# Token projections of 512 columns instead of 256, PSUM banks four/two/two, and another order of the linear attention

## The chip, the core and the metric

The kernel runs on one core of a Trainium2 chip. The metric is the device time of one launch in microseconds, from the runs' median. Engines are named as the profile names them: PE (TensorE, with PEld its weight loads), DVE (VectorE), ACT (ScalarE), POOL (GpSimd) and SP (SyncE, which issues most of the DMAs here).

## What is computed

Two transformer blocks over 512 tokens of width 1024, all in float32. The first block is a bidirectional gated linear attention (eight heads) beside a spatial gating unit; the second is a mixer (pooling beside an attention over the best 128 keys of each query), a cross attention over 256 memory tokens, and a mixture of 32 experts. Cut to the projections that the change touches:

```python
# block 1
proj = jnp.einsum('bsd,de->bse', _rmsnorm(x, norm_w), w_in)        # 10 splits of 1024 columns
(q, f_fwd, f_bwd, i, ga, u, v, gb, ma, mb) = jnp.split(proj, split_points, axis=-1)
y_a = _hgrn2_branch(q, f_fwd, f_bwd, i, ga, ...)                   # values i, output gate silu(ga)
y_b = _spatial_gating_branch(u, v, gb, ...)                        # layernorm(gelu(v))
merged = sigmoid(ma) * (y_a @ w_proj_a) + sigmoid(mb) * (y_b @ w_proj_b)
x = rmsnorm(x + merged @ w_out)
# block 2
z = rmsnorm(x) @ w_in_2                   # pooled part, q, k, v of 512 each, qi 512, ki 64, wi 8
q = apply_rope(rmsnorm(q)); k = apply_rope(rmsnorm(k)); qi = apply_rope(qi)
score = einsum(relu(qi @ ki), wi);  sel = top_k(score, 128)
x = x + concat([pool_mixer(u), attention(q, k[sel], v[sel])]) @ w_out_2
x = x + softmax(rmsnorm(h @ xattn_wq) @ rmsnorm(m @ wkv_k).T) @ (m @ wkv_v) @ xattn_wo
x = x + mixture_of_experts(rmsnorm(x))    # 2 experts per token of 32
```

## The kernel before

**Products.** A float32 product is made of three fp32r products (`mm3`, L152 to L155): both operands are split into a rounded part (`_h`) and the rest (`_l`), and high by high, high by low and low by high are summed in PSUM. There are two forms. `proj_T` (L166) holds a 128 by 128 block of the weights and moves all 512 tokens past it. `proj_tok` (L172) holds a block of 128 tokens and moves columns of the weights past it, 256 columns in the kernel before: two token tiles share one PSUM tile of 512 columns. The values of the linear attention (`gla_proj`, products `pi`), its gates (`gla_gate`, `pg`), the gating input (`sg_input`, `pv`), the memory's keys and values (`kv_unit`, `pkv`), both output projections (`pwo`, `pwo2`), the mixer's indexer queries, keys, queries and values (`qk_unit`: `pqi`, `pk`, `pq`; `v_unit`: `pvv`) and the cross attention's queries (`xq_unit`, `pxq`) have the second form. For each token tile and block of 256 columns there are 8 contraction blocks of 128, so 24 products.

**Weights.** `load_w` (L137) fetches 256 columns of a 1024-row matrix as two DMAs of 512 KB from SP's queue into a ring of two raw tiles; ACT rounds each to its high part (L131), and DVE, in two places POOL, subtracts for the low part (L132). High and low tiles have rings of two as well, so one block of weights is in use while the next one is made.

**PSUM.** The eight banks are given to three tags (L157 to L164): three `mm` for projections, three `sm` for scores, sums and the like, two `tp` for transposes.

**Order.** The source order is the priority; the framework's scheduler, which times instructions by a model of its own, writes one fixed order for each engine, and each engine then runs its own order and waits for others by semaphores. Steps that wait for other engines (the transposes of normalised queries) are postponed: they are kept in `pend` and emitted by `flush` behind later projections.

**Linear attention** (L242 to L408, main loop under `sg_input`): for each pair of heads `gla_proj` makes values, forget gates and queries, `gla_gate` the output gates of the pair; `gla_scores` builds each head's decayed scores by doublings (DVE and POOL products of decays, ACT and PE in turn), `gla_out` sums the values (`po`), normalises and gates them.

**Mixer attention.** `qk_unit` projects 256 columns of two token tiles, squares on ACT, sums on DVE (L534), takes the inverse root on POOL (L124, L125), multiplies on DVE (L536) and rotates on DVE (L649) and POOL (L653, L658). `score` (L747) adds up the indexer's scores on DVE (L757 to L760); `topk` (L763) takes the best 128 in rounds of a MAX8 (L767) and a MATCH_REPLACE8 (L768), 16 rounds for each of the query tiles 1 to 3, all on DVE. `attend` (L838) uses the selection.

**Experts.** 16 rounds of two experts, whose weights stream from HBM into buffers that earlier rounds free (L967 issues from SP).

Of the kernel before, what the change touches and what calls it, by code (L numbers as in the profile page):

```python
# [4 lines left out]
F32 = mybir.dt.float32  # L5
# [17 lines left out]
def host_consts():  # L23
    """Arrays that depend on the shapes alone: identity, masks, counters, rotary tables."""
# [37 lines left out]
def program(tc, I, out, sb, ps, dr, dbg, upto):  # L62
# [58 lines left out]
    def rstd_of(ss, n, k, eps, name):  # L121
        """(ss / n + eps) ** -0.5 on a small [128, k] tile."""
# [5 lines left out]
    def split(src, hi, lo, gain=None, eng=None):  # L128
        """hi + lo = src (times a gain per partition), hi rounded to fp32r."""
# [7 lines left out]
    def load_w(src, c0, n, name, kb=8, dst=None, eng=None):  # L137
        """Columns c0..c0+n of a [kb*128, *] matrix as fp32r hi and lo."""
# [12 lines left out]

    def mm3(o, ah, al, bh, bl, first=True, last=True):  # L152
# [13 lines left out]
    def proj_T(o, w, c0, act, kb=8, m=128):  # L166
        """o[c, t] = sum_d w[d, c0+c] act[d, t] (weights stationary)."""
# [4 lines left out]
    def proj_tok(o, act, i, w, c0, n, ks, kw=None, first=True, last=True):  # L172
        """o[t, c] over token tile i (tokens stationary), contraction blocks ks of act."""
# [6 lines left out]
    def to_T(src, i, dst, nk=8):  # L180
        """Transpose token tile src [128, nk*128] into dst hi/lo [:, k, i*128:]."""
# [13 lines left out]
    def norm_tile(dst, src, wb, name, eps=1e-6):  # L195
        """dst = rmsnorm(src) * wb for one token tile [128, 1024]."""
# [6 lines left out]
    # ================= block 1 =================  # L203
    w_in = I["w_in"][0]
    w_first = load_w(w_in, 3 * D, 256, "wi0", eng=nc.gpsimd)
# [8 lines left out]
    # forget gate bounds: lb = cumsum(softmax(lower_bounds, layers)) - first, one layer  # L214
# [25 lines left out]
    st = {}  # L240

    def gla_proj(h):  # L242
        hp, j = divmod(h, 2)
        c0 = h * 128
        if j == 0:
            wv = load_w(w_in, 3 * D + hp * 256, 256, f"wi{hp}") if hp else w_first
            for ip in range(2):
                p = pmm(f"pi{hp}_{ip}")
                for ii in range(2):
                    proj_tok(p[:, ii * 256:(ii + 1) * 256], hT, 2 * ip + ii, wv, 0, 256, range(8))  # L250
                nc.scalar.activation(V[:, 2 * ip:2 * ip + 2, hp * 256:(hp + 1) * 256],
                                     p.rearrange("p (i c) -> p i c", i=2), AF.Copy)
# [3 lines left out]
            # G slots: 0 q bwd, 1 k fwd, 2 q fwd, 3 k bwd, 4.. scores; T slots: 0 bwd, 1 fwd  # L256
# [24 lines left out]

    def gla_gate(hp):
        wg = load_w(w_in, 4 * D + hp * 256, 256, f"wga{hp}")
        gate = s4(f"gate{hp}", (128, 4, 256))
        for ip in range(2):
            p = pmm(f"pg{hp}_{ip}")
            for ii in range(2):
                proj_tok(p[:, ii * 256:(ii + 1) * 256], hT, 2 * ip + ii, wg, 0, 256, range(8))
            gv = gate[:, 2 * ip:2 * ip + 2, :]
            pv = p.rearrange("p (i c) -> p i c", i=2)  # L290
            nc.scalar.activation(gv, pv, AF.Sigmoid)
            nc.vector.tensor_tensor(gv, gv, pv, OP.mult)
        st["gate", hp] = gate

    def gla_scores(h):
        G, T, q = st[h]
        # products of the decays over blocks of m positions, at 1024 + 2 * (512 - 2 * 512 / m)
# [25 lines left out]
        def put(src, other, copy):  # L323
            """These blocks' places in the scores."""
# [5 lines left out]
        # queries with their own position's decay  # L330
# [5 lines left out]
        def widen(m):  # L336
            """from blocks of m to blocks of 2m"""
# [27 lines left out]
        # the other 128s, through the sums of keys times values that reach each of the four from either side  # L365
# [46 lines left out]
    def sg_input():  # L412
        """LayerNorm(gelu(v)) in token layout"""
        vn = a16("vn", F32, (128, 4, 1024))
        for c in range(4):
            w = load_w(w_in, 6 * D + c * 256, 256, f"wv{c}")
            for ip in range(2):
                p = pmm(f"pv{c}_{ip}")
                for ii in range(2):
# [1043 lines left out]
```

## Time and profile before

| | |
|---|---|
| median of 3 runs | 1339.22 us (1337.23 to 1342.84) |
| the profiled execution | span 1338.4 us; its time stands 0.8 us below the median |
| granted TensorE clock | 0.993 of full speed in the mean |
| PE, DVE, ACT, POOL busy | 1299.5, 774.1, 494.6, 210.3 us |
| DMA | 207.67 MB, 155 GB/s in the mean |

The stages follow one another: start and first norms to 66 us, linear attention and gating input to 375, merge and gating to 605 and memory keys and second half of the merge to 667, output projection to 713, mixer projections to 794, selection and attention to 898, mixer output and cross attention to 1071, experts to the end. An engine's busy time is read stage by stage, since each has its own limit, and an operation's duration differs from its pitch: a product's record of 0.28 us overlaps the next one's, and the distance of two starts is what a product costs.

### The profile page before, as it was taken

Reading aid. Unit: us, or ns where it says so; the run is one execution under the profiler, and the core shown is the slowest. Engines: PE = TensorE matmul, PEld = TensorE weight load, DVE = VectorE, ACT = ScalarE, POOL = GpSimd, SP = SyncE. Lnnn points to the kernel's source line nnn. Section 1 sums busy time; section 2 is a strip of 40 time slices with the busy share of each in tenths; the row PEclk is TensorE's granted clock in tenths of the full one; section 3 lists DMA queues with packets and bytes.
Section 4 is the critical chain, followed back from the end, with each engine's and each line's share of the span. In section 5 each row is a group of like instructions: output and inputs, shape, how many; then the busy total and the mean of one; then the engine's idle time right before and its main releaser. Section 6 shows DMA issues by size and latency. Waiting matters only on the chain. (4 is left out here: it accounts for less than half of the span.)

```text
span 1338.4 us, 22160 instructions
## 1 busy us (share of the span) xinstructions
PE 1299.5 (97%) x8998; PEld 1058.0 (79%) x8998; DVE 774.1 (58%) x1458; ACT 494.6 (37%) x853; POOL 210.3 (16%) x254
## 2 busy tenths in 40 slices
PE   6999999999999999999999999899999999999997
PEld 5898989899988888888899868757898846666553
DVE  4467676666662345444456479993447735555544
ACT  4355454646431343433433334355435211111110
POOL 2202011030010000100002465361011110000000
PEclk9999999999999999999999999899999999999999
DMA  6322222222423332234642322231198599999995
GB/s 187 95 81 78 65 65 84 75 64 64 158 79 95 110 106 83 80 95 142 197 141 76 95 71 64 64 108 66 64 296 305 191 309 362 359 358 357 362 361 195
DMA packets 178699, 207.67 MB, mean 155 GB/s; under 512 B 14711, under 2 KB 155767, under 8 KB 178593
## 3 DMA queue, kind: packets, MB, share of 16 engines
q1 hardware_dynamic: 171808, 197.91, 45.7%
q10 hardware_dynamic: 4624, 4.44, 1.1%
q0 software_dynamic: 2160, 3.85, 0.9%
q8 instruction: 73, 1.20, 0.4%
q14 instruction: 34, 0.27, 0.1%
HBM read 201.81 MB, written 8.39 MB: 157 GB/s over the span
## 5 line engine op out<-in xcount | busy, mean ns | idle before, releaser
L1302 PE MATMUL pgu<-gu,hgT 128*64 128x256 f32 (+1 forms) x944 | 116.3, 398 | 3.6 <-DMA gu<-in_expert_w_up 3.6
L1302 PEld LDWEIGHTS pgu<-gu,hgT 128*64 128x64 f32 x944 | 70.4, 137 | 50.0 <-issue 6.8
L353 ACT ACTIVATE qk<-G 128x512 f32<-128x512 f32 x112 | 69.1, 666 | 51.6 <-DVE G L343 51.6
L1341 DVE TENSOR_TENSOR fx<-fx,pad 128x512 f32<-128x512 f32 x128 | 77.9, 678 | 1.0 <-PE pad L1340 1.0
L1326 PE MATMUL pdn<-dn,sh 128*64 128x512 f32 x256 | 61.6, 604 | 0.0
L1307 DVE SCALAR_TENSOR_TENSOR sh<-sh,grs,pgu 128x256 f32<-128x256 f32 x16 | 7.7, 480 | 87.5 <-ACT sh L1306 87.5
L340 DVE TENSOR_TENSOR G<-G,T 128x512 f32<-128x512 f32 x56 | 39.2, 700 | 31.4 <-ACT qk L353 28.6
L1339 PE MATMUL pad<-yh,put 128*128 128x512 f32 x128 | 52.9, 417 | 0.9 <-DVE fx L1341 0.9
L1340 PE MATMUL pad<-yl,put 128*128 128x512 f32 x128 | 49.9, 394 | 0.0
L131 ACT ACTIVATE yh<-pdn 128x512 fp32r<-128x512 f32 x32 | 19.1, 597 | 73.0 <-PE pdn L1326 73.0
L1306 ACT ACTIVATE sh<-pgu,grs 128x256 f32<-128x256 f32 x16 | 7.6, 474 | 103.9 <-PE pgu L1302 103.9
L1275 POOL DMA_INDIRECT hg<-x3d,lst_i x15 | 15.1, 1008 | 184.7 <-PE thg L1284 171.4
L153 PE MATMUL pi<-wi_h,hT_h 128*128 128x256 f32 x128 | 38.1, 298 | 3.3 <-ACT hT_h L131 2.3
L304 POOL TENSOR_TENSOR T<-T 128x512 f32<-128x512 f32 (+6 forms) x56 | 31.3, 560 | 54.1 <-DVE T L271 50.4
L132 DVE TENSOR_TENSOR yl<-pdn,yh 128x512 fp32r<-128x512 f32 x32 | 22.1, 691 | 30.2 <-ACT yh L131 30.2
L343 DVE TENSOR_TENSOR G<-G,T 128x512 f32<-128x512 f32 x56 | 38.8, 692 | 0.0
L154 PE MATMUL pi<-wi_l,hT_h 128*128 128x256 f32 x128 | 38.0, 297 | 0.2 <-POOL wi_l L132 0.2
L155 PE MATMUL pi<-wi_h,hT_l 128*128 128x256 f32 x128 | 37.6, 294 | 0.0
L1326 PEld LDWEIGHTS pdn<-dn,sh 128*64 128x64 f32 x256 | 15.7, 136 | 27.5 <-issue 26.4
L153 PE MATMUL pv<-wv_h,hT_h 128*128 128x256 f32 x128 | 36.8, 288 | 0.0
L153 PE MATMUL pg<-wga_h,hT_h 128*128 128x256 f32 x128 | 36.7, 287 | 0.0
L155 PE MATMUL pv<-wv_h,hT_l 128*128 128x256 f32 x128 | 36.7, 287 | 0.0
(542 smaller groups left out, 4142.3 us busy)
## 6 DMA issues: line engine op xcount, KB each, us to landing
gu<-in_expert_w_gate SPq DMA_DIRECT2D x32, 1024.0 KB, 12.4
gu<-in_expert_w_up SPq DMA_DIRECT2D x32, 1024.0 KB, 12.6
dn<-in_expert_w_down SPq DMA_DIRECT2D x44, 512.0 KB, 9.7
wo_r<-in_w_out SPq DMA_DIRECT2D x16, 512.0 KB, 3.5
wq_r<-in_w_in SPq DMA_DIRECT2D x12, 512.0 KB, 3.7
dn<-in_expert_w_down SPq DMA_DIRECT2D x5, 1024.0 KB, 8.5
dn<-in_expert_w_down SPq DMA_DIRECT2D x20, 256.0 KB, 8.3
wi_r<-in_w_in SPq DMA_DIRECT2D x8, 512.0 KB, 4.9
```

What stands on the lines that cost most here:

```text
L153: nc.tensor.matmul(o, ah, bh, start=first, stop=False)
L154: nc.tensor.matmul(o, ah, bl, start=False, stop=False)
L155: nc.tensor.matmul(o, al, bh, start=False, stop=last)
L304: nc.gpsimd.tensor_tensor(ap_of(T, o, [[n2, 2], [1, n2]]), ap_of(T, a, [[sa, 2], [2, n2]]), ap_of(T, a + 1, [[sa, 2], [2, n2]]), OP.mult)
L340: nc.vector.tensor_tensor(ap_of(G, 0, [[512, 2], [2 * m, nb], [1, m]]), ap_of(G, 0, [[512, 2], [2 * m, nb], [1, m]]), ap_of(T, a + 1, [[sa ...
L343: nc.vector.tensor_tensor(ap_of(G, 1024 + m, [[512, 2], [2 * m, nb], [1, m]]), ap_of(G, 1024 + m, [[512, 2], [2 * m, nb], [1, m]]), ap_of( ...
L353: nc.scalar.activation(ap_of(qk, a * 512, [[2 * m, nb], [m, 2], [1, m]]), ap_of(G, a * 512, [[2 * m, nb], [1024 + m, 2], [1, m]]), AF.Copy)
L1302: nc.tensor.matmul(pg[m * a:m * a + m, c0:c0 + n], hT_[:, k, m * a:m * a + m], t[:, k, :], start=k == 0 and c0 == 0, stop=k == 7 and c0 + ...
L1326: nc.tensor.matmul(po[m * a:m * a + m, :], hd[:, f, m * a:m * a + m], dn[f][:, hs], start=f == 0, stop=f == 1)
L1339: nc.tensor.matmul(p, pi, yh[:, hs], start=True, stop=False)
L1340: nc.tensor.matmul(p, pi, yl[:, hs], start=False, stop=True)
L1341: V_.tensor_tensor(fx[:, i, hs], fx[:, i, hs], p, OP.add)
```

## The change

Every projection of the second form moves 512 columns of weights instead of 256. `load_half` fetches four contraction blocks of 512 columns (two DMAs of 512 KB, as before, but each of two blocks by 512 columns); `tok512` goes through the lower four contraction blocks for all token tiles and then through the upper four, so each token tile holds a PSUM bank of its own from its first product to its last. `pmm` has four banks and `psm` two. `done` empties a tile's bank. A gate projection serves four heads and is emptied as two halves of 256 columns. In the linear attention each `gla_scores(h)` is followed in the source by an independent projection: gates of four heads, the other values, or the gating input. The memory's keys come behind the second block of the merge and its values behind the fourth. In the mixer a unit is one token tile of 512 columns, and the indexer's scores of query tiles 1 and 2 follow the key tiles 2 and 3. Cut to its core:

```diff
+    def load_half(src, c0, b, name, eng=None, dst=None, kb=8):
+        ncol = src.shape[1]
+        if dst is None:
+            dst = (sb.tile([128, 4, 512], F32R, name=f"{name}_h{b}", tag="wh", bufs=2),
+                   sb.tile([128, 4, 512], F32R, name=f"{name}_l{b}", tag="wl", bufs=2))
+        hi, lo = dst
+        for q in range(2):
+            raw = sb.tile([128, 2, 512], F32, name=f"{name}_r{b}{q}", tag="wr", bufs=2)
+            nc.sync.dma_start(raw, bass.AP(tensor=src.tensor, offset=src.offset + c0 + (4 * b + 2 * q) * 128 * ncol,
+                                           ap=[[ncol, 128], [128 * ncol, 2], [1, 512]]))
+            split(raw, hi[:, 2 * q:2 * q + 2], lo[:, 2 * q:2 * q + 2], eng=eng)
+        return hi, lo
+
+    def tok512(src, c0, act, name, done, order=None, nt=4, eng=None, halves=None):
+        p, w = {}, halves or {}
+        for b, i in order or [(b, i) for b in range(2) for i in range(nt)]:
+            if b not in w:
+                w[b] = load_half(src, c0, b, name, eng)
+            if b == 0:
+                p[i] = pmm(f"p{name}_{i}")
+            proj_tok(p[i], act, i, w[b], 0, 512, range(4 * b, 4 * b + 4), range(4), first=b == 0, last=b == 1)
+            if b == 1:
+                done(i, p[i])
...
-        return ps.tile([128, 512], F32, name=name, tag="mm", bufs=3)
+        return ps.tile([128, 512], F32, name=name, tag="mm", bufs=4)
...
-        return ps.tile([128, 512], F32, name=name, tag="sm", bufs=3)
+        return ps.tile([128, 512], F32, name=name, tag="sm", bufs=2)
...
+        def done(i, p):
+            for a in range(2):
+                gv, pv = gates[a][:, i, :], p[:, a * 256:(a + 1) * 256]
+                nc.scalar.activation(gv, pv, AF.Sigmoid)
+                nc.vector.tensor_tensor(gv, gv, pv, OP.mult)
+        tok512(w_in, 4 * D + hp * 256, hT, f"wga{hp}", done)
...
+    gla_values(0)
     gla_proj(0)
     for h in range(0, 8, 2):
-        gla_gate(h // 2)
+        if h % 4 == 0:
+            gate_tiles(h // 2)
         gla_scores(h)
+        if h % 4 == 0:
+            gla_gate(h // 2)
+        elif h == 2:
+            gla_values(1)
+        else:
+            sg_cols(0)
         gla_out(h)
         gla_scores(h + 1)
         if h < 6:
             gla_proj(h + 2)
         else:
-            sg_input()
+            sg_cols(1)
+            sg_norm()
         gla_out(h + 1)
...
-        if c > 0:
-            kv_unit(c - 1)
+        if c % 2:
+            kv_unit(c // 2)
...
+    def k_after(i):
+        flush(2)
+        if i > 1:
+            score(i - 1)
+
+    qk_units(1024, "k", rk, True, put_k, between=k_after)
...
     score(3)
-    for c in range(2):
-        wq = load_qk(512, c, "q")
-        for ip in range(2):
-            qk_unit(wq, c, ip, "q", rq, True, put_q)
-            flush(1)
+    qk_units(512, "q", rq, True, put_q, between=lambda i: flush(1))
```

`qk_units` has the steps of `qk_unit` for one token tile and 512 columns; `load_w4` and `proj_w4` do the same for the two output projections, and `xq_done` for the cross attention's queries. Three places of the fixed orders follow; the numbers at the end of a name tell instances apart.

**PE, first head's sum over the values** (`pkv0`, `po0`; `pf` and `pf2`, `pf3` are forget gates of the next heads, `pwga` the gates of the change; rows that only repeat are left out). Before:

```order
L378 MATMUL pkv0_0_760<-V_199,kt0_748 128x128 x3
L378 MATMUL pkv0_1_767<-V_199,kt0_748 128x128 x3
L395 MATMUL po0_774<-V_199,G0_330 128x128
L154 MATMUL pf3_1_1124<-hT_l_86,wfb1_h_1061 128x512
L155 MATMUL pf3_1_1124<-hT_h_85,wfb1_l_1062 128x512
L153 MATMUL pf3_1_1124<-hT_h_85,wfb1_h_1061 128x512
```

And with the change:

```order
L180 MATMUL pwga0_3_726<-wga0_l1_740,hT_h_95 128x512
L181 MATMUL pwga0_3_726<-wga0_h1_739,hT_l_96 128x512
L404 MATMUL pkv0_0_663<-V_209,kt0_651 128x128 x3
L404 MATMUL pkv0_1_670<-V_209,kt0_651 128x128 x3
L421 MATMUL po0_813<-V_209,G0_344 128x128
L425 MATMUL po0_813<-sm0_652,G0_344 128x128
L423 MATMUL po0_813<-sm0_652,G0_344 128x128
L179 MATMUL pf2_1_1024<-hT_h_95,wfb1_h_990 128x512
L180 MATMUL pf2_1_1024<-hT_l_96,wfb1_h_990 128x512
```

Before, projections of the next pair of heads stand between the sums; with the change the sums follow the gates' last products with no projection between, and the next projection `pf2_1` needs an `mm` bank, of which the gate tiles hold all four until they are emptied.

**PE, start of the first output projection** (`pwo`, weights `wo`). Before:

```order
L154 MATMUL pkv3_5781<-wkv3_l_5772,mmT_4972 128x256
L155 MATMUL pkv3_5781<-wkv3_h_5771,mmT_4972 128x256
L153 MATMUL pwo0_0_5881<-wo0_h_5839,mT_h_5753 128x256
L154 MATMUL pwo0_0_5881<-wo0_l_5840,mT_h_5753 128x256
L155 MATMUL pwo0_0_5881<-wo0_h_5839,mT_l_5754 128x256
```

And with the change:

```order
L180 MATMUL pwkv1_1_5108<-wkv1_l1_5122,mmT_4412 128x512
L179 MATMUL pwo0_0_0_5225<-woa_h0_5183,mT_h_5157 128x512
L179 MATMUL pwo0_0_1_5251<-woa_h0_5183,mT_h_5157 128x512
L180 MATMUL pwo0_0_0_5225<-woa_l0_5184,mT_h_5157 128x512
L181 MATMUL pwo0_0_0_5225<-woa_h0_5183,mT_l_5158 128x512
L180 MATMUL pwo0_0_1_5251<-woa_l0_5184,mT_h_5157 128x512
L181 MATMUL pwo0_0_1_5251<-woa_h0_5183,mT_l_5158 128x512
```

Before, one token tile runs through all its blocks in a row; with the change two tiles take turns at the pace of the weight blocks, here after 12 products of each 512 KB.

**DVE, first selection** (`m8_1_r` is round r of query tile 1; `sc1` and `ksc` are scores, `qn` the queries' norms). Before:

```order
L768 MATCH_REPLACE sc1_6401<-m8_1_2_7479,sc1_6401 128x256
L759 SCALAR_TENSOR_TENSOR ksc_6400<-rl2_3_7109,wi_6728,ksc_6400 128x384
L536 TENSOR_TENSOR qn0_0_7246<-pq0_0_7197,qn0_0_r_7250 128x512
L767 MAX m8_1_3_7482<-sc1_6401 128x8
L759 SCALAR_TENSOR_TENSOR ksc_6400<-rl2_4_7114,wi_6728,ksc_6400 128x384
```

And with the change:

```order
L797 MAX m8_1_0_6329<-sc1_5545 128x8
L569 TENSOR_TENSOR qn2_6279<-pwq_2_6175,qn2_r_6283 128x512
L798 MATCH_REPLACE sc1_5545<-m8_1_4_6341,sc1_5545 128x256
L567 TENSOR_REDUCE qn3_q_6312<-qn3_6310 128x8
L132 TENSOR_TENSOR wvv_l1_6389<-wvv_r10_6390,wvv_h1_6388 128x1024
L797 MAX m8_1_5_6344<-sc1_5545 128x8
L132 TENSOR_TENSOR wvv_l1_6389<-wvv_r11_6394,wvv_h1_6388 128x1024
L789 SCALAR_TENSOR_TENSOR ksc_5544<-rl2_3_6055,wi_5776,ksc_5544 128x384
L798 MATCH_REPLACE sc1_5545<-m8_1_5_6344,sc1_5545 128x256
L569 TENSOR_TENSOR qn3_6310<-pwq_3_6188,qn3_r_6314 128x512
```

Before, one of the four query units is normalised within the first six rounds; with the change all four are, the last (`qn3`) behind round 5 counted from 0.

## Rows read from the trace of the kernel before

**Rows 1.** Page, part 1: busy us, share of the span and instructions of each engine.
```profile
PE 1299.5 (97%) x8998; PEld 1058.0 (79%) x8998; DVE 774.1 (58%) x1458; ACT 494.6 (37%) x853; POOL 210.3 (16%) x254
```
**Rows 2.** Windows by stage: us, busy us (x) of PE, PEld, DVE, ACT, POOL; PEclk, DMA, GB/s.
```profile
66.00:375.00 309.00, 309.00 (x2850) 280.94 (x2849) 210.16 (x347) 164.09 (x275) 45.95 (x77) 1.00 0.27 84
...
794.00:898.00 104.00, 98.41 (x549) 73.05 (x547) 99.19 (x247) 45.70 (x95) 52.12 (x34) 0.95 0.21 64
898.00:1071.00 173.00, 171.33 (x1338) 148.84 (x1338) 98.12 (x308) 72.53 (x171) 24.85 (x37) 1.00 0.55 187
1071.00:1243.00 172.00, 170.88 (x1080) 98.75 (x1078) 88.96 (x177) 23.26 (x44) 14.13 (x14) 1.00 1.05 350
```
**Rows 3.** Timeline of PE: first of 384 pwo products, and the instruction behind the last.
```profile
666.81 0.28 PE L153 MATMUL pwo<-wo_h,mT_h 128*128 128x256 f32 x1
...
713.03 0.38 PE L185 MATMUL tp_h2T_h<-csq,xr 128*128 128x128 f32 x2
```
**Rows 4.** Timeline of PE: first of 96 products pmb and ppb, instruction behind the last.
```profile
605.10 0.40 PE L153 MATMUL pmb<-hT_h,wmb_h 128*128 128x512 f32 x1
...
626.89 0.49 PE L556 MATMUL tkm<-csq,km 128*128 128x128 f32 x3
```
**Rows 5.** Lines of ACT, 60 to 375: busy us, mean ns of one.
```profile
L131 ACT ACTIVATE wga_h<-wga_r 128x1024 fp32r<-128x1024 f32 x6 | 6.0, 1051 | 0.1
...
L334 ACT ACTIVATE B<-pd 128x256 f32<-128x256 f32 x8 | 3.0, 379 | 0.0
```
**Rows 6.** Page, part 6: DMA issues, KB each, us from issue to landing.
```profile
wo_r<-in_w_out SPq DMA_DIRECT2D x16, 512.0 KB, 3.5
```
**Rows 7.** Timelines of PE and DVE: first key product, first score, start and end of the selections.
```profile
749.05 0.40 PE L153 MATMUL pk<-wk_h,h2T_h 128*128 128x256 f32 x2
...
780.59 0.83 DVE L757 TENSOR_SCALAR sc<-rl,wi 128x256 f32<-128x256 f32 x1
...
793.60 0.43 DVE L767 MAX8 m<-sc 128x8 f32<-128x256 f32 x1
...
897.09 1.22 DVE L769 TENSOR_SCALAR ksc<-ksc 128x512 f32<-128x512 f32 x1
```
**Rows 8.** Lines of DVE, 793.6 to 898.3: busy us, mean ns of one.
```profile
L759 DVE SCALAR_TENSOR_TENSOR ksc<-rl,wi,ksc 128x384 f32<-128x384 f32 (+1 forms) x14 | 11.1, 795 | 0.0
L767 DVE MAX8 m<-sc 128x8 f32<-128x256 f32 x16 | 6.7, 422 | 0.2
L768 DVE MATCH_REPLACE8 sc<-m,sc 128x256 f32<-128x256 f32 x16 | 6.5, 407 | 0.0
...
L132 DVE TENSOR_TENSOR wvv_l<-wvv_r,wvv_h 128x1024 fp32r<-128x1024 f32 x4 | 5.6, 1428 | 0.0
...
L536 DVE TENSOR_TENSOR qn<-pq,qn_r 128x512 f32<-128x512 f32 x4 | 2.7, 680 | 1.0 <-POOL qn_r L125 1.0
```
**Rows 9.** Timeline of POOL: two key units, four instructions each (one left out of each).
```profile
777.29 0.20 POOL L124 TENSOR_SCALAR kn_r<-kn_q 128x8 f32<-128x8 f32 x1
777.57 1.65 POOL L125 TENSOR_TENSOR kn_r<-kn_r,mhalf 128x8 f32<-128x8 f32 x1
...
782.09 1.34 POOL L658 TENSOR_TENSOR ko_a<-ko_a,kn 128x512 f32<-128x512 f32 x1
784.40 1.10 POOL L124 TENSOR_SCALAR kn_r<-kn_q 128x8 f32<-128x8 f32 x1 [0.97 <-DVE kn_q L534]
785.59 2.50 POOL L125 TENSOR_TENSOR kn_r<-kn_r,mhalf 128x8 f32<-128x8 f32 x1
...
791.39 1.36 POOL L658 TENSOR_TENSOR ko_a<-ko_a,kn 128x512 f32<-128x512 f32 x1 [0.72 <-DVE ko_a L649]
```
**Rows 10.** Waits of DVE, 700 to 960: us in total, times, longest.
```profile
DVE kn L536 <- POOL kn_r L125: 12.0, 4, 4.1
```
**Rows 11.** Lines, 1005.6 to 1019, cross attention: busy us, mean ns of one.
```profile
L1047 ACT ACTIVATE xpe<-pxs,xmx 128x256 f32<-128x256 f32 x13 | 6.0, 476 | 1.0 <-DVE xmx L1043 0.9
```
**Rows 12.** Chain of waits, 1240 to 1330: start us, us, what.
```profile
1302.06 12.76 DMA gu<-in_expert_w_up
```

More of the change, by code (lines that the diff above doesn't have):

```diff
@@ L204, in program @@
     w_in = I["w_in"][0]
-    w_first = load_w(w_in, 3 * D, 256, "wi0", eng=nc.gpsimd)
+    w_first = {b: load_half(w_in, 3 * D, b, "wi0", nc.gpsimd) for b in range(2)}
     hT = (a16("hT_h", F32R), a16("hT_l", F32R))
@@ L240, in program, with gla_values @@
     st = {}
+    def gla_values(b):
+        vs = slice(b * 512, b * 512 + 512)
+        tok512(w_in, 3 * D + b * 512, hT, f"wi{b}", lambda i, p: nc.scalar.activation(V[:, i, vs], p, AF.Copy),
+               halves=None if b else w_first)
     def gla_proj(h):
@@ L280, in gla_proj, with gate_tiles @@
                 nc.vector.scalar_tensor_tensor(q, p, float(128 ** -0.5), s, OP.mult, OP.mult)
+    def gate_tiles(hp):
+        for a in range(2):
+            st["gate", hp + a] = s4(f"gate{hp + a}", (128, 4, 256))
     def gla_gate(hp):
[L283 to L293, printed above, removed]
+        gates = [st["gate", hp + a] for a in range(2)]
+        def done(i, p):
+            for a in range(2):
+                gv, pv = gates[a][:, i, :], p[:, a * 256:(a + 1) * 256]
+                nc.scalar.activation(gv, pv, AF.Sigmoid)
+                nc.vector.tensor_tensor(gv, gv, pv, OP.mult)
+        tok512(w_in, 4 * D + hp * 256, hT, f"wga{hp}", done)
     def gla_scores(h):
@@ L610, in program @@
             nc.sync.dma_start(xt[ii], I["x"][0, i * 128:(i + 1) * 128, :])
[L611 to L612 removed]
+        for c in range(2):
             for ii in range(2):
[L614 to L616 removed]
+                p = pmm(f"pwo{c}_{ip}_{ii}")
+                proj_w4(p, [mT], 2 * ip + ii, wo[c])
+                residual(2 * ip + ii, c, 512, p, xt[ii])
         flush()
@@ L707, in program, with qk_units, done, turn @@
-    del pend[2:]
-    flush()
-    pend.extend(turns)
-    for c in range(2):
-        qk_unit(wqi[c], c, 1, "qi", rope, False, put_qi)
-        flush(2)
+    def qk_units(off, name, tab, norm, put, order=None, between=None):
+        def done(i, p):
+            if norm:
+                x = head_norm(p, f"{name}n{i}", 8, 64)
+            else:
+                x = s4(f"{name}x{i}")
+                nc.scalar.activation(x[:, 1, :], p, AF.Copy)
+            ro = rotate(x, tab, i, 1, 8, f"{name}o{i}", None)
+            def turn():
+                tp = ptp(f"t{name}{i}")
+                for pp in range(4):
+                    nc.tensor.transpose(tp[:, pp * 128:(pp + 1) * 128], ro[:, pp * 128:(pp + 1) * 128], ident)
+                put(tp.rearrange("p (a t) -> p a t", a=4), i)
+            pend.append(turn)
+            if between:
+                between(i)
+        tok512(w_in2, off, h2T, f"w{name}", done, order)
@@ new lines, in put_qi, with put_k, put_q, late_rows @@
+    def put_qi(tp, i):
+        nc.scalar.activation(qiT[:, :, i * 128:(i + 1) * 128], tp, AF.Copy)
+    def put_k(tp, i):
+        nc.scalar.activation(kT[:, :, i * 128:(i + 1) * 128], tp, AF.Copy)
+    def put_q(tp, i):
+        nc.scalar.activation(qT[:, :, i * 128:(i + 1) * 128], tp, AF.Copy)
+    turns = pend[:]
+    del pend[:]
+    def late_rows(i):
+        if i == 0:
+            for f in turns:
+                f()
+    qk_units(2048, "qi", rope, False, put_qi, [(0, 0), (0, 1), (1, 0), (1, 1), (0, 2), (0, 3), (1, 2), (1, 3)],
+             late_rows)
@@ L884, in fill_first @@
     def fill_first():
-        for c in range(2):
-            v_unit(c, 1)
+        for i in range(2, 4):
+            v_units([(0, i), (1, i)])
             yield
@@ L915, in mix_out @@
             nc.sync.dma_start(xt[ii], x1d[i * 128:(i + 1) * 128, :])
-        for c in range(4):
-            p = pmm(f"pwo2{c}_{ip}")
+        for c in range(2):
             for ii in range(2):
-                proj_tok(p[:, ii * 256:(ii + 1) * 256], (pcat[:, 0], pcat[:, 1]), 2 * ip + ii, wo2[c], 0, 256,
-                         range(4), last=False)
-                proj_tok(p[:, ii * 256:(ii + 1) * 256], (acat[:, 0], acat[:, 1]), 2 * ip + ii, wo2[c], 0, 256,
-                         range(4), range(4, 8), first=False)
-            for ii in range(2):
-                residual(2 * ip + ii, c, 256, p[:, ii * 256:(ii + 1) * 256], xt[ii])
-            yield
+                p = pmm(f"pwo2{c}_{ip}_{ii}")
+                proj_w4(p, [(pcat[:, 0], pcat[:, 1]), (acat[:, 0], acat[:, 1])], 2 * ip + ii, wo2[c])
+                residual(2 * ip + ii, c, 512, p, xt[ii])
+                yield
         for ii in range(2):
```

171 lines of the change are left out of this document (52 added, 119 removed).

## The prediction

> **What bounds the kernel now.** First the page's busy times: PE works 1299.5 of 1338.4 us and nothing else comes near [rows 1], so a shorter stream of products shortens the program wherever PE ends last, and only there. Which stages those are stands in the table by stage [rows 2]: PE is busy for the whole of the linear attention (309.00 of 309), and nearly so (170.88 of 172) in the experts; in the stage of the selections, 794 to 898, DVE has 99.19 of 104 us, and PE's granted clock, 1.00 in the other stages shown, is 0.95. There the chain is DVE's, and it begins where the first best-of round starts (793.60) and ends with the last mask (897.09 + 1.22) [rows 7]. The tail of the experts waits for weights: one fetch of 12.76 us stands in the chain of waits as late as 1302 [rows 12], and the transfers run full from 1071 (350 GB/s) but at 187 GB/s between 898 and 1071 [rows 2]: there they wait for buffers that earlier stages free, so I let the end move with the start of the experts.
>
> What a product costs is read from two long runs without a stop, start to start, not from durations, which overlap. 384 products of 256 columns take 713.03 − 666.81 = 46.22 us, 120.4 ns each [rows 3]; 96 products of 512 columns take 626.89 − 605.10 = 21.79 us, 227.0 ns each [rows 4].
>
> **The change part by part.**
>
> *Width, the gain.* There are 3072 products of 256 columns: 384 each of pi, pg, pv, pwo and pwo2, 192 each of pkv, pqi, pk, pq, pvv and pxq. They become 1536 of 512. A pair cost 2 × 120.4 = 240.8 ns and costs 227.0, so 13.8 ns, and 1536 × 13.8 = **21.2 us** of PE: 7.9 in the linear attention and gating input (576 pairs), 1.3 in pkv, 2.6 in pwo, 1.3 in pqi, 4.0 in pk, pq and pvv (288 pairs), 2.6 in pwo2, 1.3 in pxq. Both pitches are the columns at 2.4 GHz (106.7 and 213.3 ns) and 13.7 ns more, so what is saved is one fixed part of every second product. The 512-column rows are of the form that holds weights; that the form that holds tokens has the same pitch is taken from them. Bounds of the width's gain: 0 (a pitch of 240.8) and 21.2.
>
> The Trainium skill ("TensorE: Matmul & The Clock Gate", section Back-to-back issue gap) gives N/2.4 + 2.5 ns as the distance of isolated products, and says that the loads of the held operand come on top in a real stream; by the formula a pair would save one 2.5 ns, 3.8 us in all. The trace has the form but not the size, 13.7 ns in the place of 2.5.
>
> *Under the selections, not earned.* The 4.0 us of pk, pq and pvv lie beside DVE's chain [rows 7]. Cost **4.0**, bounds 0 and 4.
>
> *Gates and banks in the linear attention.* A gate projection now holds all four mm banks. In the new order the first head's sums follow with no projection between, and the next projection must wait for a bank. Emptying is 8 pieces of 256 columns on ACT for a gate of four heads; the nearest row is 0.379 us for such a piece [rows 5], so 8 × 0.379 = 3.0 us, twice in the kernel, behind splits of weights of 1.051 us [rows 5] that ACT's order puts first. If PE's small sums cover it, nothing is lost; if both gates stall in full, 6. I take one, **3.0** (0 to 6). That ACT has more pieces is free: it is busy 164 of 309 us there. Better filling of the doublings' waits is the possible gain: PE counts as busy throughout [rows 2], so I put it at nothing.
>
> *Weight ring.* One half of a projection's weights is now 4 blocks by 512 columns, still two DMAs of 512 KB into two raws, so bytes and the count of issues on SP stay the same. With two token tiles in turn, pkv (two tiles by nature) and the first half of pwo use 12 products, 12 × 0.227 = 2.7 us, per 512 KB, against a landing of 3.5 [rows 6] and a rounding of 1.051 [rows 5], 4.6 us until a raw is free again. Two raws in flight give one per 2.3 us, so it is at the edge. **2.0** (0 to 8, which is 4 us on each side of the merge's end). Behind a late block there stands all of PE's order: the second tile needs the same block.
>
> *Start.* The first values need both halves of their weights; the second takes the place of a forget gate's fetch. No row prices that; POOL is the splitter and mostly idle there. 0 (−1 to 2).
>
> *Selections.* Let T be the first key product (749.05) [rows 7]. Before, the first score came at T + 31.5 and the first round at T + 44.5, 13.0 later. Now every key tile ends late, since all four go through the lower half first: tile 0 after 60 products, T + 13.6, the others 2.7 us apart. Squares and sums take a bit over 1 us; the inverse root and rotation of a unit cost POOL 6.1 us in a quiet unit (777.29 to 782.09 + 1.34) and 8.35 beside DVE (784.40 to 791.39 + 1.36) [rows 9]. DVE waited for exactly this before: 12.0 us in four waits for the root [rows 10]. The first score stands behind the third unit's product on DVE: T + 15 + 2 × 6.1 + 1.9 = T + 29, or T + 15 + 2 × 8.35 + 3.6 = T + 35, then about 4 us (a product of 0.68, a rotation of like size, two splits [rows 8]). So T + 33 to T + 39, and the first round 13.0 later, T + 46 to T + 52. I take T + 47, 2.5 late, of which 1 comes back because two of four value splits (1.428 each [rows 8]) now run ahead of the first round. **1.5** (−4 to 6). Queued behind a late root on DVE are all 48 rounds; who waits for them is the attention, and behind it PE.
>
> *Cross attention with two score banks.* A score bank is held through a reduction and two exponentials of 0.476 us [rows 11], eight banks in all, where three could be held before and two can now. **1.0** (0 to 3). The same two banks serve the expert rounds; their tail waits for weights anyway [rows 12], so 0.
>
> *Sum.* 21.2 − 4.0 − 3.0 − 2.0 − 1.5 − 1.0 = 9.7; 1338.4 − 9.7 = 1328.7. The profiled execution stands 0.8 below the median, so **1329**. Bounds of this case by half of the unknowns each way: 1323 to 1335.
>
> **The rivals.**
>
> *All of it arrives*: the scheduler's order covers the banks, the ring keeps pace and DVE's chain starts no later, or earlier. 1338.4 − 21.2 + 0.8 = **1318**, 1312 to 1323 with a few us from better filling or a chain 4 earlier. For it: PE has room for no wait before 749, and a wait of the ring is at most as deep as the raws. Against: 4.0 us lie under DVE.
>
> *No change*: the selections start at T + 52 and wait for roots within the rounds, 10 late rather than 1.5. 1338.4 − 21.2 + 4.0 + 3.0 + 2.0 + 10 + 1.0 + 0.8 = **1338**. For it: POOL's contended unit. Beside it stands a case of pitch, not of waits: the wide product of the token form takes a larger fixed part, 20.6 ns in place of 13.7, and half of the gain goes, 10.6, of which 2.0 would have lain under DVE: 1338.4 − 10.6 + 2.0 + 3.0 + 2.0 + 1.5 + 1.0 + 0.8 = 1338 again. Against it: the fixed part is the same at both sizes measured. The Trainium skill's small fixed part (same page and section) would bring the time still closer to no change.
>
> *Slower, POOL's chain holds the rounds.* All four query units' products now stand within the first selection's first six rounds; before, one did. Up to the last one's multiplication DVE has 6 rounds of 0.83 (5.0 us), four scores of 0.795, two splits of 1.428, three products of 0.68 and two sums, about 15 us [rows 8], so it comes there at T + 62. If every unit takes POOL 8.35 us, the seven ahead end at T + 15 + 58.5, the last root 3.6 later, T + 77: DVE stands 15 us, behind a start 5 late. 1338.4 + 20 − (21.2 − 4.0 − 3.0 − 2.0 − 1.0) + 0.8 = **1348**. The rival begins to cost where the last query's root comes after T + 62, and gives a slower kernel from about T + 75. Against it: quiet units take 6.1, by which the same sum gives T + 15 + 42.7 + 1.9 = T + 60, just in time.
>
> That the change does not do what it says is excluded: the orders show products of 512 columns at every place.
>
> **How the numbers follow.** The measurement can tell about 0.5%, 6.7 us, from no change: faster is below 1332.5, slower above 1345.9. My forecast has 0.45 (0.33 of it below 1332.5, 0.12 above), all of it 0.25, no change 0.11 and its case of the pitch 0.03, POOL's chain 0.12, and 0.04 for something slower that I don't name, such as expert rounds that two score banks stretch. Faster 0.33 + 0.25 = 0.58; same 0.12 + 0.11 + 0.03 = 0.26; slower 0.12 + 0.04 = 0.16. The range from 1314 to 1345 leaves out the slow cases and the quickest part of the second, a little under 2 in 10.
>
> **What would show it.** In the profile after: PE's first pwo product to the transposes behind the last should take 192 × 227 = 43.6 us where 46.2 stood, if the ring keeps pace; pitch of a pwga or pwq product 227 ns, and if it is 240 the gain is void. The linear attention's end should come some 5 us earlier. A stall of PE at the next heads' forget gates, released by ACT's gate pieces, would show the banks. The first MAX8 should start 46 to 52 us after the first key product, and the last mask end about 150 after it; waits of DVE for qn_r of several us would be the slow rival. I am wrong if the linear attention, the one stage that PE fills and that holds the largest share, doesn't shorten, or if the selections move by more than 6 us.

## The result and the profile after

The changed kernel takes **1356.09 us** (median of 4 runs, 1355.35 to 1356.66), the kernel before 1338.22 beside it: ratio 1.0125, 95% interval 1.0103 to 1.0147, so slower by 16.7 us. The forecast was 1329 and faster; 1356 lies above the range's 1345.

Times of different runs are compared below by their ratio to the kernel before, which was measured beside each of them; each ratio has its interval, and is put in microseconds against 1339.

The page of the changed kernel, engines, answers to [rows 1]: PE is busy for 3 us less with 1536 products fewer, but for 96% of a longer span.

```profile
PE 1296.4 (96%) x7462; PEld 977.8 (72%) x7462; DVE 768.3 (57%) x1448; ACT 498.2 (37%) x861; POOL 204.9 (15%) x256
```

The table by stage answers to [rows 2]. It has the same borders in time, although the work has slid by some 10 us.

```profile
66.00:375.00 309.00, 304.56 (x2290) 248.93 (x2289) 203.75 (x351) 160.24 (x277) 48.35 (x82) 0.99 0.24 75
...
794.00:898.00 104.00, 95.76 (x357) 61.23 (x356) 94.43 (x234) 43.42 (x91) 45.96 (x32) 0.91 0.18 58
898.00:1071.00 173.00, 167.10 (x930) 127.75 (x929) 99.40 (x267) 78.70 (x179) 25.65 (x39) 0.97 0.52 177
1071.00:1243.00 172.00, 164.86 (x1124) 98.37 (x1121) 86.85 (x212) 22.02 (x44) 13.16 (x13) 1.00 1.02 341
```

In the linear attention PE now pauses (304.56 of 309), and the experts' PE falls from 170.88 to 164.86 of 172. To see where time went, the stages are better cut at events. Each column gives the time from the event above to this one, in the profiled executions (all read from timelines):

| stage, up to | before | after |
|---|---|---|
| first pu product (linear attention, first half of the merge) | 462.4 | 473.3 |
| first pwo product | 204.4 | 204.0 |
| last pki product | 82.0 | 77.2 |
| first MAX8 | 44.8 | 48.7 |
| last MAX8 | 100.3 | 100.4 |
| first cross-attention score | 111.8 | 106.5 |
| first expert product | 64.9 | 70.3 |
| end | 267.9 | 274.4 |

The gain is seen where PE streams: −4.8 in the output projection and the indexer's queries, −5.3 behind the selections. Four stages lose: +10.9, +3.9, +5.4, +6.5. The linear attention, which the forecast wanted some 5 us shorter, is the first of them.

**The width is paid.** Timeline of PE, first of 48 products of the memory's keys and values (`pwkv`) and the instruction behind the last: 677.34 − 666.46 = 10.88 us, 226.7 ns each, against [rows 4] with its 227.0.

```profile
666.46 0.39 PE L179 MATMUL pwkv<-wkv_h,mmT 128*128 128x512 f32 x1
...
677.34 0.39 PE L179 MATMUL pwo<-woa_h,mT_h 128*128 128x512 f32 x1
```

**The first hole**, head 0. Timelines of PE, ACT and DVE (start, duration, engine):

```profile
102.26 1.50 PE L404 MATMUL pkv<-V,kt 128*128 128x128 f32 x12
108.20 0.77 PE L421 MATMUL po<-V,G 128*128 128x128 f32 x2 [4.45 <-DVE sm L409]
...
102.50 2.00 ACT L131 ACTIVATE wff_h<-wff_r 128x1024 fp32r<-128x1024 f32 x2 [2.96 <-issue]
...
103.59 2.36 DVE L132 TENSOR_TENSOR wff_l<-wff_r,wff_h 128x1024 fp32r<-128x1024 f32 x2 [7.19 <-ACT wff_h L131]
105.87 0.34 DVE L409 SCALAR_TENSOR_TENSOR sm<-sm,T,pkv 128x128 f32<-128x128 f32 x1
106.13 1.41 DVE L318 TENSOR_TENSOR gate<-gate,pwga 128x256 f32<-128x256 f32 x4
107.45 0.60 DVE L409 SCALAR_TENSOR_TENSOR sm<-sm,T,pkv 128x128 f32<-128x128 f32 x2
```

The waiting product (L421) reads only V and G. What it lacks is its place: `po` is a score tile, and both score banks hold `pkv` until DVE's L409 has read them. L409 in turn stands on DVE behind the split of a forget gate's weights, whose first step on ACT starts (102.50) only as the gates' last product ends and frees their weight tile, and then behind four pieces of the gates' own emptying (L318, 1.41 us). So PE stands for 4.45 us, with the next projection queued behind `po`.

**The second hole**, head 7: timelines of PE and DVE.

```profile
387.81 0.80 PE L423 MATMUL po<-sm,G 128*128 128x128 f32 x2 [4.11 <-DVE sm L409]
...
382.37 0.34 DVE L409 SCALAR_TENSOR_TENSOR sm<-sm,T,pkv 128x128 f32<-128x128 f32 x1
382.63 4.87 DVE L459 SCALAR_TENSOR_TENSOR vn<-vn,ln_r,lnb 128x1024 f32<-128x1024 f32 x4
387.41 0.34 DVE L409 SCALAR_TENSOR_TENSOR sm<-sm,T,pkv 128x128 f32<-128x128 f32 x1
```

Here it is a sum that PE reads, not a bank: it stands behind four operations of the layer norm on DVE. At the end of each of the two holes (from 107.4 and 387.3, 0.8 and 0.5 us before PE goes on) the granted clock falls to half, 1.2 GHz, for 6.8 us; the windows around them, with 0.83 in the column PEclk:

```profile
100.00:120.00 20.00, 15.55 (x85) 13.36 (x83) 13.63 (x29) 12.00 (x25) 1.21 (x2) 0.83 0.17 52
...
380.00:400.00 20.00, 13.72 (x63) 11.40 (x62) 14.47 (x20) 6.24 (x8) 1.21 (x2) 0.83 0.35 119
```

**The cross attention.** PE waits twice for over 1 us, where the kernel before has no wait over 0.4 us in that stage. Timeline of PE:

```profile
1015.16 0.91 PE L1021 MATMUL txq<-csq,xqn 128*128 128x128 f32 x4 [2.63 <-DVE xqn L569]
1017.94 2.08 PE L1044 MATMUL pxs<-kvm,qm 128*128 128x256 f32 x4 [1.87 <-ACT xpe L1052]
```

The first is a wait for the last normalised queries. In the second, `pxs` reads nothing of `xpe`, whose exponentials read an earlier score tile: it is a wait for a score bank.

**The expert rounds** take 16.4 us each where they took 15.8. Waits of PE from 1080 to the end (us in total, times, longest): two bubbles of 0.3 us, 14 times each.

```profile
PE pdn L1331 <- DVE fx L1346: 4.6, 14, 0.4
PE pgu L1307 <- DVE hgT L1298: 4.3, 14, 0.4
```

### The profile page after: what moved, and what is told of

The parts are those of the page before. It is cut to its first block, busy times and chain, and to the rows that moved or that the text cites. A ratio compares the mean times of both kernels' runs of the same rounds, so it can differ in the third digit from the quotient of the medians.

```text
span 1354.8 us, 19026 instructions
## 1 busy us (share of the span) xinstructions
PE 1296.4 (96%) x7462; PEld 977.8 (72%) x7462; DVE 768.3 (57%) x1448; ACT 498.2 (37%) x861; POOL 204.9 (15%) x256
## 4 chain that ended last, share of the span: by engine, by line
PE 82%; DVE 7%; DMA 4%; issue 3%; ACT 2%; POOL 1%; SPq 0%; DVEq 0%; ACTq 0%; POOLq 0%
PE pgu L1307 8%; PE pdn L1331 3%; PE pl L345 2%; PE pad L1344 2%; PE pf L181 2%; PE pf L179 2%; PE pf L180 2%; PE pad L1345 2%; PE pwo L179 2%; PE pwo L181 2%; PE pwo L180 2%; PE pwv L179 1%; DVE fx L1346 1%; PE pwv L181 1%; PE pwv L180 1%
## 5 line engine op out<-in xcount | busy, mean ns | idle before, releaser
L1307 PEld LDWEIGHTS pgu<-gu,hgT 128*64 128x64 f32 x944 | 67.8, 137 | 55.1 <-DVE hgT L1298 16.7
L1331 PE MATMUL pdn<-dn,sh 128*64 128x512 f32 x256 | 58.5, 598 | 5.9 <-DVE fx L1346 4.6
L345 PEld LDWEIGHTS pl<-qk 128*64 128x64 f32 x896 | 29.4, 137 | 13.5 <-issue 8.3
L345 PE MATMUL pl<-qk 128*64 128x64 f32 x896 | 35.1, 226 | 0.0
L385 DVE COPY_PREDICATED B<-cmask,pl 128x256 f32<-128x256 uint8 x48 | 21.3, 444 | 19.7 <-PE pl L345 19.3
L1344 PEld LDWEIGHTS pad<-yh,put 128*128 128x128 f32 x128 | 24.0, 188 | 11.7 <-issue 6.4
L1345 PEld LDWEIGHTS pad<-yl,put 128*128 128x128 f32 x128 | 24.1, 188 | 4.1
```

The source lines that it names most:

```text
L345: nc.tensor.matmul(p[64 * j:64 * j + 64, c * 64:c * 64 + 64], kt[:, k0:k0 + 64], qt[:, q0:q0 + 64], start=True, stop=True)
L1307: nc.tensor.matmul(pg[m * a:m * a + m, c0:c0 + n], hT_[:, k, m * a:m * a + m], t[:, k, :], start=k == 0 and c0 == 0, stop=k == 7 and c0 + ...
L1331: nc.tensor.matmul(po[m * a:m * a + m, :], hd[:, f, m * a:m * a + m], dn[f][:, hs], start=f == 0, stop=f == 1)
L1344: nc.tensor.matmul(p, pi, yh[:, hs], start=True, stop=False)
L1345: nc.tensor.matmul(p, pi, yl[:, hs], start=False, stop=True)
```

## The experiments

Theory A in what follows: losses come from what stands in the fixed orders around the sums, the score bank costs in the expert rounds alone. Theory B: the missing score bank costs in every stage.

**e1_before_banks**, the kernel before with the banks of the change:

```diff
-        return ps.tile([128, 512], F32, name=name, tag="mm", bufs=3)
+        return ps.tile([128, 512], F32, name=name, tag="mm", bufs=4)
-        return ps.tile([128, 512], F32, name=name, tag="sm", bufs=3)
+        return ps.tile([128, 512], F32, name=name, tag="sm", bufs=2)
```

> The kernel before with four mm banks and two sm banks, nothing else. Theory A (holes come from what stands in the fixed orders, banks cost only in the expert rounds): first pu product stays at 462 us (464 at most), expert rounds go from 15.8 to about 16.4 us, time 1338 + 6.6 = about 1345. Theory B (two score banks are what costs in every stage): first pu near 470 too, cross attention 3 to 5 us longer, time 1350 to 1356. Rival: no effect at all, 1338.

Measured: 1361.67, ratio 1.0167 (1.0136 to 1.0198), **+22 us**, more than either theory gave. The first pu product comes at 467.7 (+5.3), the selections take 105.8 (+5.5), the next stage 114.6 (+2.8), the experts 274.4 (+6.5), with the two bubbles of the changed kernel (waits of PE from 1080):

```profile
PE pdn L1326 <- DVE fx L1341: 4.5, 14, 0.4
PE pgu L1302 <- DVE hgT L1293: 4.3, 14, 0.4
```

Theory B holds in the main: without width and with the old source, the new numbers of banks cost more than the whole change. Two things stay open. The cross attention takes 65.3 us against 64.9, so the 3 to 5 more that theory B gave it did not come. And of the linear attention's 5.3 only 0.9 is seen as a wait of PE (60 to 480). The numbers of banks also change the orders that the scheduler writes, here from the first head's sums on, so the step holds both.

**e3_pdn_mm**, the changed kernel, down products in the other tag:

```diff
-            po = psm(f"pdn{name}_{half}")
+            po = pmm(f"pdn{name}_{half}")
```

> The changed kernel, but the experts' down products take their bank from mm (four) and no longer from sm (two). If two sm banks pace the expert rounds: rounds back from 16.4 to 15.8 us, time 1356 - 6.6 = about 1349.5. If the rounds are paced by DVE or by the weights: 16.4 stays, 1356.

Measured: 1352.73, ratio 1.0099 (1.0071 to 1.0127), 3.5 us less than the change by the ratios, with overlapping intervals, where 6.6 were expected. The rounds are back at 15.8 and the last stage at 268.7 (−5.7). Both bubbles are gone and the wait for weights is back, as before the change [rows 12]; waits of PE from 1080:

```profile
PE pgu L1307 <- DMA gu<-in_expert_w_up: 3.7, 3, 2.2
```

**e5_gate_first**, the changed kernel:

```diff
+        if h % 4 == 0:
+            gla_gate(h // 2)
         gla_scores(h)
-        if h % 4 == 0:
-            gla_gate(h // 2)
```

> The changed kernel with the gate projection ahead of the scores of heads 0 and 4 in the source, as before, instead of behind them. Theory A: the hole of 4.4 us ahead of the first head's sums and the 6.8 us of half clock behind it go, 4.4 + 3.4 = 7.8 less: about 1348. Rival: the hole only moves to another head: 1354 to 1357.

Measured: 1349.99, ratio 1.0073 (1.0047 to 1.0099), 6 us less by the medians. The first hole is gone: forget-gate products now stand between `pkv0` and `po0` in PE's order. The holes at head 7 are gone too, and 2.6 us of waits for the layer norm (`pmx`) stand in their place. The half clock at 107 is gone, the one near 387 comes at 380, and the first pu comes at 463.8 in place of 473.3; part of these 9.5 is given back later.

**e4_banks33**, three score banks for the changed kernel. Four token tiles at a time don't fit into three mm banks, so projections go by pairs:

```diff
-        for b, i in order or [(b, i) for b in range(2) for i in range(nt)]:
+        for b, i in order or [(b, 2 * j + i) for j in range(nt // 2) for b in range(2) for i in range(2)]:
...
-        return ps.tile([128, 512], F32, name=name, tag="mm", bufs=4)
+        return ps.tile([128, 512], F32, name=name, tag="mm", bufs=3)
-        return ps.tile([128, 512], F32, name=name, tag="sm", bufs=2)
+        return ps.tile([128, 512], F32, name=name, tag="sm", bufs=3)
```

> The changed kernel with three mm and three sm banks, for which each wide projection goes by pairs of token tiles (both weight halves for tiles 0 and 1, then for 2 and 3). Theory A and B both: expert rounds 15.8 (-6.6), cross attention shorter by some 3, and, as projections then stand between the sums of heads 0 and 7, the two holes of PE and the two half-clock stretches behind them go (-18): 1356 - 28 = about 1328. Rival: both weight halves are held to the end of each projection, so the next one's weights come late at eight places, 2 to 3 us each: about 1345 to 1350.

Measured: 1324.64, ratio 0.9879 (0.9848 to 0.9909): **16 us faster than before**, 33 than the change. The first pu comes at 458.6, the first MAX8 38.7 us after the last pki product (44.8 before, 48.7 in the change), though the last one 145.9 (145.0 and 149.1), and rounds take 15.8. Over 60 to 480 the sums keep PE waiting for 1.1 us (first fence, waits of PE), and both windows of the holes are full (second, windows):

```profile
PE po L425 <- DVE sm L409: 1.1, 2, 0.6
```

```profile
100.00:120.00 20.00, 20.00 (x161) 16.33 (x161) 17.62 (x33) 14.81 (x26) 1.56 (x2) 1.00 0.33 103
...
380.00:400.00 20.00, 20.00 (x110) 17.23 (x109) 9.73 (x14) 7.12 (x10) 0.00 (x0) 1.00 0.25 79
```

**e6_pairs42**, e4 with the banks of the change (its only edit the two numbers back):

> The changed kernel with four mm and two sm banks as it is, but every wide projection by pairs of token tiles, as in e4_banks33. It tells banks from order. If the banks are what the two differ by: expert rounds 16.4 (+6.5), the rest +8 to +14, 1324.6 + 15 to 20 = 1340 to 1345. If it was the order by pairs (one gate tile at a time holds a bank, so projections lie between the sums): the linear attention ends as in e4_banks33 (first pu near 459) and only the experts' 6.5 are lost, 1331.

Measured: 1358.59, ratio 1.0129 (1.01 to 1.0159), 33 us slower than e4 and no better than the change. So with these banks pairs in place of halves do nothing; I had expected 15 to 20 us from the banks, and they cost 33. The linear attention has holes again, among them two of 4.1 and 4.6 us (waits of PE, 60 to 480):

```profile
PE po L423 <- DVE sm L409: 5.5, 2, 4.1
PE po L421 <- DVE sm L409: 4.6, 1, 4.6
```

**e14_pairs32 and e15_before32** take the score bank away and leave it unused, from e4 and from the kernel before:

```diff
-        return ps.tile([128, 512], F32, name=name, tag="sm", bufs=3)
+        return ps.tile([128, 512], F32, name=name, tag="sm", bufs=2)
```

> The kernel of e4_banks33 with one score bank less and that bank left unused: three mm, two sm, two tp. If the third score bank alone makes the 34 us between e4_banks33 and e6_pairs42: 1355 to 1360. If the fourth mm bank did harm (an order that the scheduler wrote for it): near 1335 to 1345. If the fourth mm bank helped: above 1362.

> The kernel before with one score bank less and that bank left unused: three, two, two. If the score bank alone makes the 22.6 us of e1_before_banks: 1358 to 1365. If the fourth mm bank had a part in them: 1345 to 1352.

Measured: e14 1340.47, ratio 1.0004 (0.9992 to 1.0016); e15 1357.49, ratio 1.0139 (1.0121 to 1.0156). The third score bank is worth 17 us in the wide kernel (0.9879 to 1.0004) and 19 in the one before, in each together with the order that the scheduler writes for it: e4 and e14 differ in PE's order from the first head on. The second step is the surprise: giving the idle bank to the projections makes the wide kernel **17 us slower** (1.0004 to 1.0129). In the kernel before the same step reads +4 (1.0139 to 1.0167), within the intervals. With that bank the scheduler writes another order: in e14 a whole gate tile's 24 products stand behind the first nine of `po4`, in e6 they are all ahead, and PE is busy 39.10 of 40 us from 240 to 280 in e14 and 35.37 in e6. No run changes the banks and keeps the order, so how much of either step is waiting for a bank and how much is another order is not shown. The expert rounds take 16.0 us in e14 and e15 and 16.4 in e6 and e1, and the stage 269.3 in the first two and 275.1 and 274.4 in the others (267.9 before): two score banks alone cost the experts 1.4, and the rest came with the fourth mm bank. Only one of the two bubbles stands in e14 (waits of PE from 1070):

```profile
PE pgu L1307 <- DVE hgT L1298: 4.3, 14, 0.4
```

**e13_431 and e12_341** give a third score bank to the change, and a fourth to the best kernel, at the cost of a transpose bank (`tag="tp", bufs=1`).

> The changed kernel with its third score bank given back at the cost of a transpose bank: four, three, one; order by halves over four token tiles as it is. If the missing score bank is the cause: expert rounds back to about 15.8 unless the single transpose bank stretches them, no hole ahead of the first head's sums, 1356 - 15 to 25 = 1331 to 1341 less what one transpose bank costs. If holding four mm banks at once is the cause: 1350 to 1360.

> The kernel of e11_best with a fourth score bank instead of the second transpose bank. If score banks still bind: 1305 to 1312. If three are enough: no gain, and the single transpose bank costs some us, 1316 to 1330.

Measured: e13 1363.14, ratio 1.0176 (1.016 to 1.0191); e12 1368.94, ratio 1.021 (1.0182 to 1.0238). Both are slower than the kernels they are made from (by 7 and 49 us), e12 far beyond both of its expectations, so a transpose bank, with the order that went with it, costs more than a score bank gives there. As a test of the cause e13 is inconclusive, though in the linear attention the waits for L409 shrink, as expected of a third score bank, to one of 1.8 us. Waits of PE in e12's experts show the new bubble, once a round:

```profile
PE thg L1293 <- DVE hgT L1302: 11.8, 15, 0.8
```

**e7_33_gate** is e4 with the edit of e5.

> The kernel of e4_banks33 with the gate projection ahead of the scores of heads 0 and 4. If a hole in PE's order is still left at head 0 or 4: 3 to 6 less, about 1320. If three score banks and pairs had closed it already: 1323 to 1326.

Measured: 1321.02, ratio 0.9852 (0.9824 to 0.988), 3.6 us below e4 by the medians, with overlapping intervals. The trace has the first pu at 454.7 (−3.9).

**e8_33_xq** is e4 with the cross attention's query transposes early:

```diff
         if i == 0:
             for f in turns:
                 f()
+        else:
+            flush(2)
```

> The kernel of e4_banks33 with the first cross-attention query transposes emitted as soon as the third token tile is normalised, not behind all four. If the end of the query projection is where the cross attention lost its 3.2 us (68.1 against 64.9 from the first score to the first expert product): 2 to 3 less, 1322. If the rest of the stage's order loses it: 1324 to 1326.

Measured: 1318.81, ratio 0.984 (0.981 to 0.9869). From the first cross-attention score to the first expert product 65.6 us, in e4 68.1. The experts take 266.9, in e4 270.0, which is one long round at e4's end (20.5 us, in e8 17.4) and not traced to the edit. The intervals of the two overlap.

**e10_split256** prices the width: e8 with each wide product as two.

```diff
-            proj_tok(p[i], act, i, w[b], 0, 512, range(4 * b, 4 * b + 4), range(4), first=b == 0, last=b == 1)
+            for c in range(2):
+                proj_tok(p[i][:, c * 256:(c + 1) * 256], act, i, w[b], c * 256, 256, range(4 * b, 4 * b + 4), range(4),
+                         first=b == 0 and c == 0, last=b == 1 and c == 1)
```

(and the same in `proj_w4`)

> The kernel of e8_33_xq with each wide product issued as two of 256 columns, banks, order by pairs, loads and emptying kept. It prices the width alone. By the two pitches 1536 pairs cost 21.2 us more, of which some 4 lie under the selections: 1319 + 17 = 1336. If e9_wo_only is right in that width is worth little in this program: 1319 to 1325.

Measured: 1342.96, ratio 1.003 (1.0017 to 1.0042), 25 us slower than e8 (24.2 by the medians). The width is worth what the pitches say, within the uncertainty of some 4 us: 25.4/1536 = 16.5 ns a pair where I had 13.8. From the last pki product to the first cross-attention score e10 takes 256.2 us and e8 243.5, 12.7 for the 576 pairs in between, whose pitch gives 7.9, so nothing is missing there. The selections themselves did not get shorter: up to the last MAX8 e10 takes 141.3 and e8 146.9, and the gain comes behind it; why there is not shown.

**e9_wo_only**, the kernel before with the two output projections wide (`load_w4`, `proj_w4` of the change):

> The kernel before (three, three, two banks) with only the two output projections at 512 columns, 768 products of 256 replaced by 384. It measures the width by itself: 384 pairs at 13.8 ns are 5.3 us, so 1338.5 - 5.3 = about 1333, with the first output projection 43.6 us long where it took 46.2. If a ring that is at its edge gives half of it back: 1335 to 1337.

Measured: 1340.43, ratio 0.9998 (0.9983 to 1.0013): nothing. The first output projection is shorter, 712.53 − 667.98 = 44.55 us against 46.22, though not 43.6. From the first pu product to the first cross-attention score it gains 2.7; the cross attention behind it is 2.1 longer (67.0), and 1.2 were lost ahead of the edit. Why these 384 pairs gain nothing where 5.3 us were forecast is not settled: what is lost lies outside the widened products, and the cross attention's order, which e8 improved, is one place.

**e11_best** is e4 with the edits of e7 and e8.

> Three, three, two banks, pairs, the gate projection ahead of the scores, and the query transposes of the cross attention early: the edits of e7_33_gate (-3.6) and e8_33_xq (-5.8) on e4_banks33 together. If they lie in different stages and add up: about 1315. If both take from the same slack behind the start of the experts: 1318 to 1319.

Measured: 1318.09, ratio 0.9847 (0.9832 to 0.9862). The first pu comes at 454.2, 4.6 earlier than in e8, and the first expert product hardly earlier than in e8 (1048.8 and 1049.5): from the first MAX8 to the first cross-attention score it takes 208.4 us, in e8 204.8. The two edits don't add up. e8 and e11 are the fastest, some 20 us under the kernel before and 37 under the change.

## Why the prediction was wrong

Put one after the other, the runs lead from the kernel before to the change (ratio times 1339, so each step is uncertain by about 4 us):

| step | run | against before |
|---|---|---|
| order of the source, loads of 512 columns, pairs, query transposes early; banks as before, still 256-column products | e10 | +4 |
| products of 512 columns | e8 | −21 |
| query transposes late, as in the change | e4 | −16 |
| one score bank less | e14 | +0.5 |
| that bank given to the projections | e6 | +17 |
| halves over four tiles in place of pairs | after | +17 |

- **Width, 21.2 us: right**, 25 measured. That 4.0 of it lie unearned under the selections is not borne out: up to the last MAX8 nothing is gained, as the prediction said, but the whole stretch up to the cross attention shortens by 12.7, more than all its pairs' 7.9. The fixed part per product, 13.7 ns by the rows, stands. The 2.5 ns that the Trainium skill ("TensorE: Matmul & The Clock Gate", Back-to-back issue gap) gives for isolated products would, as an estimate, have made 3.8 us, and these products disagree. For a real stream that section of the Trainium skill counts the weight loads too, and calls its formula too short at small and too long at large sizes; here both sizes stand above it, 120.4 and 227.0 ns.
- **Banks: the step that failed.** The prediction put the score banks at "**1.0** (0 to 3)" in the cross attention and "so 0" in the expert rounds, and priced the fourth mm bank only by the gates' emptying, "**3.0** (0 to 6)": 4.0 together. Measured together, e4 against e6, they cost 33 us, 17 with the score bank taken away and 17 with that bank given to the projections, each with the order that the scheduler wrote for it. That is more than the 27 us by which the forecast was off. I looked for users of the score bank in the cross attention alone. The score blocks of the doublings (`pd`, `pl`), the sums `pkv` and `po`, the indexer's scores, the attention's scores, the experts' down products and half of their additions share that tag, and in the stalls shown for the linear attention and the experts work on DVE sets when PE may go on. The place of the gates' stall was right (head 0), its kind only in part: PE waits for a score bank, not for the gates' banks, but 1.41 us of the gates' emptying stand on DVE ahead of the operation that frees it. In the cross attention, where the prediction did look, the third bank buys little: PE's waits for ACT's exponentials are 1.9 us in the change and 2.4 in e4 with three score banks.
- **The cover of the expert rounds was too thin.** I let the wait for weights hide them: it stood in the last three rounds of 16 (3.6 us), and a bubble comes in every round. 0.6 us more in each of 14 rounds is 8.4; the waits for weights are gone, and the stage is 6.5 longer.
- **The half clock was left out.** A hole costs itself, 4.1 to 4.45 us here, and then most of 6.8 us at half clock; e5 was expected to win 3.4 from one such stretch, and no run prices it alone.
- **The linear attention**, which by the prediction would show it wrong if it did not shorten, got 10.9 us longer.
- **Selections, 1.5 late: the size is near.** The first MAX8 comes 48.5 us after the first key product (803.23 − 754.78; forecast 46 to 52, before 44.5), and the last mask ends 152.7 after it (forecast about 150, before 149.3), so 3.4 late. DVE waited less for POOL's roots than before [rows 10]; waits of DVE, 740 to 910:

```profile
DVE kn L569 <- POOL kn_r L125: 6.2, 3, 2.8
```

- **The slower rival was the wrong one.** POOL's chain did not hold the rounds: no wait of DVE for a query's root is listed there. "Expert rounds that two score banks stretch" got 0.04 with others that I didn't name, and it was a part of the loss.
- **Weight ring, 2.0:** `pwkv` lost nothing (226.7 ns); the first output projection took 44.7 us (722.05 − 677.34) in place of 43.6, so 1.1.

## What to carry to other kernels

Before a buffer is moved from one tag to another, list every user of the tag that loses it, and ask at each how long a tile is held and by which engine; a bank that is short in a loop costs in every round of it, here 0.6 us in 14 rounds. Price such a move by itself, with the order that it brings, since here it hid a gain of 25 us; the width kept with the old banks, with projections by pairs of tiles, is the faster kernel. And where a scheduler writes the order, a resource that is added can cost time as well.

## What was not expected of the hardware

With each of the two holes of PE in the linear attention (4.45 us, and 4.11 with a shorter one of 1.28 ahead) the granted clock went to half for 6.8 us, of which all but the first 0.8 and 0.5 us lie behind the hole. Within the spans of the profiled executions the half-clock stretches add up to 49.3 us in the changed kernel, 18.2 before and 15.3 in e11.

In the wide kernel eight banks in use were slower than seven when the eighth went to the projections: e14, with one bank idle, beats e6 by 17 us. The Trainium skill ("Perfetto Trace Analysis", Matmul Optimizations) advises to see that all eight are in use. Here it depends on what the eighth serves: as a score bank (e4) it gains 17 us on e14, and with each use went another order. The Trainium skill's hint that the same gap, repeated, can mean too few buffers for the next tile (same page, Optimization Strategy) fits the bubbles of 0.3 us, 14 of each kind: in e3, where the down products take their bank from the tag with four, both are gone.
